# Intra-chunk decay masks of a state-space scan: rows read back from DRAM and masked by GpSimd selects, instead of float32r matmuls on TensorE

## The chip, the core and the metric

One NeuronCore of a Trainium2 chip runs the whole program as a single launch. Its engines are TensorE (PE, with weight loads as PEld), VectorE (DVE), ScalarE (ACT), GpSimd (POOL) and SyncE (SP, which here only issues DMAs). Each engine runs its own instructions in order and waits on semaphores for the others. The metric is the device time of one execution in microseconds (us).

## The reference, cut to what matters

One layer: adaLN and an input projection split into three head groups (a bidirectional Mamba-2 scan, pooling, neighbourhood attention), an output projection, then a PEER expert FFN and a final norm. The sequence has 512 tokens, that is 4 chunks of 128; the scan has 16 heads and two directions. Only this part of the scan is touched:

```python
def segsum(a):
    t = a.shape[-1]
    cs = jnp.cumsum(a, axis=-1)
    diff = cs[..., :, None] - cs[..., None, :]
    mask = jnp.tril(jnp.ones((t, t), dtype=bool))
    return jnp.where(mask, diff, -jnp.inf)
...
    lmat = jnp.exp(segsum(a))
    cb = jnp.einsum('bclhn,bcshn->bhcls', cc, bc)
    y_diag = jnp.einsum('bhcls,bcshp->bclhp', cb * lmat, xd)
```

For every chunk, head and direction a 128x128 matrix of log decays is needed, whose entry is the difference of two cumulated sums, with the wrong triangle at minus infinity. It goes through an exponential, is multiplied with `cb`, and weighs the tokens of the chunk.

## The kernel before, in words

The stage that the change touches runs from about 216 to 368 us of the span. It is written out by hand as 61 numbered steps (`at(step, f, ...)`, run in order of steps, and within a step in the order of the calls); every engine receives its instructions in that order. Three things are interleaved in it:

- The z, v and q projections: 16 pieces of weights (`p_load`, `p_split`), each loaded by SP into one of 3 `wraw` buffers, split by ACT (`wh`, L212) and DVE (`wl`, L215) into a high and a low float32r part, and used by 3 matmuls of 512 columns for each pair of operands (`mm3`, L222 to L224). About one fourth of a piece is done in each step.
- The chunk states (`st_in`, `st_mm`, `st_add`): DVE forms `xd` (L919) in one step, TensorE multiplies it in the next (L926), DVE adds in the one after that (L937), all in a chain.
- The within-chunk work. For chunk `c` (0 to 3) and unit `u` (0 to 3; four heads each), with `b = 4 + 10 * c`: `u_mm` in step `b+2u+1`, `u_exp` in `b+2u+2`, `u_mul` in `b+2u+3`, `u_diag` in `b+2u+5`. So there are 16 units, each two steps apart, and a pause of two steps between chunks.

In `u_mm` TensorE makes the masked cumulated sums of four heads, for both directions, in two PSUM banks: a product of a 128x128 matrix `steps[x]` with `rows` (128 x 2048, the identity times -2^100 in 112 partitions, and the cumulated sums, split in high and low, in the other 16), then a small product with `negs` for the last 16 columns (L969, L970). `u_exp` has ACT take the exponential with a bias for each head (L979, L982; 8 instructions of 128 columns). `u_mul` is two tensor_tensor instructions on DVE (L987: the two directions are added; L988: times `cb`). `u_diag` is four matmuls of 64 columns (L997). GpSimd has one instruction for each chunk in this stage, `y_init` (L1003). The constants `steps` (GpSimd, L912), `rows` (ACT, L901, and a DMA, L903), `idr` and `negs` (DVE, L905 and L909) are made once, at the stage's beginning. The cumulated sums come from two small matmuls, are split by ACT and DVE (L767, L768) and written to DRAM as `cs_d` (L770).

The last 20 steps (about 326 to 368 us) hold the gating, the norm and the transposes of the scan's output, and the q projection. Attention, the output projection and the FFN follow; they are not touched.

Of the kernel before, what the change touches and what calls it, by code (L numbers as in the profile page):

```python
# [7 lines left out]
F32 = mybir.dt.float32  # L8
F32R = mybir.dt.float32r
# [3 lines left out]
AF = mybir.ActivationFunctionType  # L13
ALU = mybir.AluOpType
# [3 lines left out]
P = 128  # L18
# [12 lines left out]
MASKED = -1.0e30  # L31
# [14 lines left out]


C_ID, C_U, C_L, C_SU, C_SL, C_ONE = 0, 128, 256, 384, 512, 640
C_X, NCST = 768, 784


def _consts():
    c = np.zeros((P, NCST), np.float32)
    k = np.arange(P)[:, None]
    m = np.arange(P)[None, :]
    c[:, C_ID:C_ID + P] = k == m
    c[:, C_U:C_U + P] = k <= m
    c[:, C_L:C_L + P] = k >= m
    c[:, C_SU:C_SU + P] = k > m
    c[:, C_SL:C_SL + P] = k < m  # L60
    c[:, C_ONE:C_ONE + P] = 1.0
    c[:, C_X:C_X + 8] = (k - 112 == m[:, :8]) | (k - 120 == m[:, :8])
    c[:, C_X + 8:C_X + 9] = k < 112
    return c


# [93 lines left out]
def build(tc, A, out, dbg=None):  # L160
    nc = tc.nc
    V, S, G, PE = nc.vector, nc.scalar, nc.gpsimd, nc.tensor
# [104 lines left out]
    cst = pers.tile([P, NCST], F32, name="cst")  # L267
    nc.scalar.dma_start(cst[:, 0:P], A["cst"][:, 0:P])
    ident = cst[:, C_ID:C_ID + P]
    U_in, L_in = cst[:, C_U:C_U + P], cst[:, C_L:C_L + P]  # L270
    SU, SL, ONE = cst[:, C_SU:C_SU + P], cst[:, C_SL:C_SL + P], cst[:, C_ONE:C_ONE + P]
# [483 lines left out]
    def decays(specs):  # L755
# [4 lines left out]
        for i, (_, _, t) in enumerate(specs):  # L760
            tc.keep_in_program_order(S.activation(t.rearrange("p t h -> p (t h)"), ps[:, i * HC:(i + 1) * HC], AF.Exp))
        return ps
    csT = [ad1.tile([NX * NH, 2, P], F32R, name=f"csT{i}") for i in range(2)]
    pcs = psG.tile([P, 512], F32, name="acc")[0:NX * NH, 0:2 * P].rearrange("p (d t) -> p d t", d=2)
    for d, m in enumerate((U_in, L_in)):
        tc.keep_in_program_order(PE.matmul(pcs[:, d, :], an[:, d, 0:NX, :].rearrange("p t h -> p (t h)"), m, start=True, stop=True))
    S.activation(csT[0], pcs, AF.Copy)  # L767
    V.tensor_tensor(csT[1], pcs, csT[0].bitcast(F32), ALU.subtract)  # L768
    for i in range(2):
        nc.scalar.dma_start(cs_d[i].rearrange("d p t -> p d t"), csT[i].bitcast(F32))  # L770
    decays([(SU, 0, enF), (SL, 1, enB), (ONE, 0, toF)])
    pin = decays([(ONE, 1, toB), (U_in, 0, inF), (L_in, 1, inB)])
    for d in range(2):
# [34 lines left out]
    def at(step, f, *a):  # L808
        plan.setdefault(step, []).append((f, a))
# [86 lines left out]
    def half_of(g):  # L896
        return slice(g * 512, (g + 1) * 512), slice(g * 8, (g + 1) * 8)
    SB = m1.tile([P, 4, D], F32, name="SB")
    rows = m1.tile([P, NH * P], F32R, name="rows")
    for i in range(4):  # L900
        S.activation(rows[0:112, i * 512:(i + 1) * 512].rearrange("p (h t) -> p h t", t=P), ident[0:112].unsqueeze(1).broadcast_to([112, 4, P]),  # L901
                     AF.Copy, scale=-2.0 ** 100)
    nc.scalar.dma_start(rows[112:P].bitcast(F32), cs_d.rearrange("i d (c h) t -> (i d c) (h t)", c=NX))  # L903
    idr = m1.tile([P, P], F32R, name="idr")
    V.tensor_copy(idr, ident)  # L905
    negs, steps = [], []
    for d, m in enumerate((SU, SL)):
        negs.append(m1.tile([P, 16], F32R, name=f"neg{d}"))
        V.tensor_scalar(negs[d], m[:, 112:P], -1e30, None, ALU.mult)  # L909
    for x in range(8):  # L910
        steps.append(m1.tile([P, P], F32R, name=f"steps{x}"))
        G.tensor_scalar(steps[x], (SL, SU)[x // 4], cst[:, C_X + 8:C_X + 9], cst[:, C_X + x:C_X + x + 1], ALU.mult, ALU.add)  # L912
    st, tmp = {}, {}


# [45 lines left out]
        for g in range(2):  # L961
            cbm[g, "r"] = cb[:, g, :]

    def u_mm(c, u):
        un[c, u] = []
        for d in range(2):
            ps = psM.tile([P, 512], F32, name="mm") if d else psT.tile([P, 4, P], F32, name="pt").rearrange("p a b -> p (a b)")
            x = 4 * d + c
            PE.matmul(ps, steps[x], rows[:, u * 512:(u + 1) * 512], start=True, stop=False)  # L969
            PE.matmul(ps.rearrange("p (a b) -> p a b", a=4)[:, :, 112:P], idr, negs[d].unsqueeze(1).broadcast_to([P, 4, 16]), start=False, stop=True)  # L970
            un[c, u].append(ps)

    def u_exp(c, u):
        pf, pb = un[c, u]
        t1 = m2.tile([P, 4, P], F32, name="t1", bufs=3)
        t2 = m2.tile([P, 4, P], F32, name="t2")
        for j in range(4):
            h = u * 4 + j
            S.activation(t1[:, j, :], pf[:, j * P:(j + 1) * P], AF.Exp, bias=ncs[0][:, c, h:h + 1])  # L979
        for j in range(4):  # L980
            h = u * 4 + j
            S.activation(t2[:, j, :], pb[:, j * P:(j + 1) * P], AF.Exp, bias=ncs[1][:, c, h:h + 1])  # L982
        un[c, u] = [t1, t2]

    def u_mul(c, u):
# [84 lines left out]
    for c in range(4):  # L1070
        b = U0 + UP * c
        at(b - 2, c_mm, c)
        at(b - 1, c_copy, c)
        for u in range(4):
            at(b + 2 * u + 5, u_diag, c, u)
            at(b + 2 * u + 1, u_mm, c, u)
            at(b + 2 * u + 2, u_exp, c, u)
            at(b + 2 * u + 3, u_mul, c, u)
        at(b + 1, y_init, c)
        at(b + 8, y_add, c, 0)  # L1080
        at(b + 12, y_add, c, 1)
# [1154 lines left out]
```

## Time and profile before

| | |
|---|---|
| runs of the kernel before | 1728.9, 1728.95, 1731.65 us, median 1728.95 |
| the profiled execution | 1730.5 us, of which the span from the first to the last instruction is 1728.7 us |
| mean granted TensorE clock | 0.997 |
| the touched stage | about 216 to 368 us of the span |

In the profile's rows a line stands for one group of instructions: line of the kernel, engine, operation, what it writes and reads, shape. In a timeline, the first column is the start in us from the span's start, the second the duration in us; the bracket at the end is the idle time of the engine before it and what ended it. In a table of windows, each engine has its busy us and the number of instructions.

### The profile page before, as it was taken

The numbers are of one execution on the slowest core, as the hardware profiler recorded it, in microseconds if no ns is written. First come the engines' busy times: TensorE is split into PE (matmuls) and PEld (weight loads), VectorE is DVE, ScalarE is ACT, GpSimd is POOL, SyncE is SP. The second block draws the span as 40 slices with busy tenths as digits, with TensorE's granted clock in tenths as the row PEclk, the third lists the DMA queues.
The fourth block names the chain that finished last, engine by engine and source line by source line (L and its number), as shares of the span: only waits on it lengthen the run. The fifth ranks groups of instructions, "written<-read, shape, count | busy, mean of one in ns | idle before, by whom it ended". The sixth has DMA issues, their size and how long they took to land.

```text
span 1728.7 us, 26484 instructions
## 1 busy us (share of the span) xinstructions
PE 1709.1 (99%) x9620; PEld 1482.9 (86%) x9620; DVE 1399.3 (81%) x2672; ACT 836.8 (48%) x1511; POOL 364.0 (21%) x283
## 2 busy tenths in 40 slices
PE   9999999999999999999999999999999999999998
PEld 7888777776789889999999999888888888888886
DVE  6688467886546599888989997988988989889886
ACT  5442345556535333556676764444444444444444
POOL 0003210012236444132121211222221212211200
PEclk9999999999999999999999999999999999999999
DMA  9457532375536434587999999999999999999972
GB/s 374 131 152 233 163 98 73 129 256 172 171 118 190 119 115 131 169 295 258 340 339 356 341 328 343 391 396 368 389 369 378 372 414 380 382 371 379 390 274 108
DMA packets 195634, 464.88 MB, mean 269 GB/s; under 512 B 14600, under 2 KB 118760, under 8 KB 177536
## 3 DMA queue, kind: packets, MB, share of 16 engines
q1 hardware_dynamic: 146976, 260.03, 43.6%
q0 software_dynamic: 21136, 144.83, 21.9%
q10 hardware_dynamic: 27392, 58.34, 9.1%
q8 instruction: 75, 1.23, 0.3%
q14 instruction: 55, 0.45, 0.1%
HBM read 409.92 MB, written 55.32 MB: 269 GB/s over the span
## 4 chain that ended last, share of the span: by engine, by line
PE 81%; DVE 8%; ACT 4%; DMA 3%; issue 2%; ACTq 1%; POOL 0%; SPq 0%; DVEq 0%; POOLq 0%
PE pv L224 10%; PE pv L223 10%; PE pv L222 10%; PE pu L224 7%; PE pu L222 7%; PE pu L223 7%; PE acc L222 5%; PE acc L223 5%; PE acc L224 5%; DMA act_d<-act 3%; DVE wl L215 2%; PE acc L461 1%; PE acc L466 1%; PE acc L463 1%; PE sps L1180 1%
## 5 line engine op out<-in xcount | busy, mean ns | idle before, releaser
L215 DVE TENSOR_TENSOR wl<-wraw,wh 128x1024 fp32r<-128x1024 f32 x295 | 361.3, 1236 | 97.6 <-ACT wh L212 95.9
L212 ACT ACTIVATE wh<-wraw 128x1024 fp32r<-128x1024 f32 x328 | 342.1, 1054 | 194.8 <-PE acc L223 75.6
L222 PE MATMUL pu<-u2h,wh 128*128 128x368 f32 x1008 | 336.8, 334 | 1.5 <-ACT act L1530 1.3
L224 PE MATMUL pu<-u2h,wl 128*128 128x368 f32 x1008 | 332.3, 330 | 1.5 <-DVE wl L215 1.5
L223 PE MATMUL pu<-u2l,wh 128*128 128x368 f32 x1008 | 331.8, 329 | 0.0
L224 PE MATMUL pv<-wh,wwl 128*128 128x512 f32 x768 | 299.3, 390 | 0.0
L223 PE MATMUL pv<-wl,wwh 128*128 128x512 f32 x768 | 299.1, 390 | 0.0
L222 PE MATMUL pv<-wh,wwh 128*128 128x512 f32 x768 | 299.0, 389 | 0.1
L1809 POOL DMA_INDIRECT row<-in_peer_uv,idxG x128 | 159.3, 1245 | 615.7 <-DVE accG L1823 577.0
L222 PEld LDWEIGHTS pu<-u2h,wh 128*128 128x128 f32 x1008 | 189.6, 188 | 3.4 <-ACT act L1530 1.7
L224 PEld LDWEIGHTS pu<-u2h,wl 128*128 128x128 f32 x1008 | 189.6, 188 | 2.8 <-DVE wl L215 2.7
L223 PEld LDWEIGHTS pu<-u2l,wh 128*128 128x128 f32 x1008 | 189.7, 188 | 1.4
L212 ACT ACTIVATE wwh<-gd 128x384 fp32r<-128x384 f32 x124 | 65.1, 525 | 242.8 <-DVE gd L2054 227.5
L224 PEld LDWEIGHTS pv<-wh,wwl 128*128 128x128 f32 x768 | 144.1, 188 | 30.4 <-DVE wwl L215 0.3
L222 PEld LDWEIGHTS pv<-wh,wwh 128*128 128x128 f32 x768 | 144.2, 188 | 29.3 <-ACT wwh L212 0.5
L223 PEld LDWEIGHTS pv<-wl,wwh 128*128 128x128 f32 x768 | 144.1, 188 | 29.1
L1823 DVE SCALAR_TENSOR_TENSOR accG<-row,wG,accG 128x1024 f32<-128x1024 f32 x127 | 162.4, 1279 | 1.6
L1814 DVE CUSTOM_DVE_ANT_0 row<-row,u2G 128x1024 f32<-128x1024 f32 x128 | 154.8, 1218 | 0.0
L1897 ACT ACTIVATE stg<-gdps 128x512 f32<-128x512 f32 x96 | 100.9, 1159 | 19.8 <-ACT act L1530 14.1
L215 POOL TENSOR_TENSOR wl<-wraw,wh 128x1024 fp32r<-128x1024 f32 x33 | 79.1, 2402 | 101.7 <-ACT wh L212 71.0
L1530 ACT ACTIVATE act<-pu 128x368 f32<-128x368 f32 x90 | 42.7, 474 | 107.7 <-PE pu L224 52.4
L215 DVE TENSOR_TENSOR wwl<-gd,wwh 128x384 fp32r<-128x384 f32 x124 | 68.9, 556 | 21.9 <-ACT wwh L212 21.9
(493 smaller groups left out, 3016.1 us busy)
## 6 DMA issues: line engine op xcount, KB each, us to landing
wraw<-in_peer_ut SPq DMA_DIRECT2D x128, 512.0 KB
wraw<-in_peer_uv SPq DMA_DIRECT2D x128, 512.0 KB
gd<-gd_d SPq DMA_DIRECT2D x15, 1536.0 KB
gd_d<-stg ACTq DMA_DIRECT2D x11, 2048.0 KB
wraw<-in_w_in SPq DMA_DIRECT2D x40, 512.0 KB
acl<-act_d SPq DMA_DIRECT2D x92, 184.0 KB
act_d<-act ACTq DMA_DIRECT2D x90, 184.0 KB
wraw<-in_w_out SPq DMA_DIRECT2D x16, 512.0 KB
```

What stands on the lines that cost most here:

```text
L212: S.activation(hi, full, AF.Copy)
L215: (eng or V).tensor_tensor(lo, full, hi.bitcast(F32), ALU.subtract)
L222: PE.matmul(ps, ah, bh, start=start, stop=False)
L223: PE.matmul(ps, ah, bl, start=False, stop=False)
L224: PE.matmul(ps, al, bh, start=False, stop=stop)
L461: PE.matmul(px, h[:, k, :], uh[:, k, :], start=s, stop=False)
L463: PE.matmul(px, h[:, k, :], ul[:, k, :], start=False, stop=False)
L1530: S.activation(act, pu[:, :TU], AF.Gelu)
L1809: G.indirect_dma_start(out=rows[k], out_offset=None, in_=A["peer_uv"], in_offset=bass.IndirectOffsetOnAxis(ap=idxG[:, k:k + 1], axis=0))
L1814: V.tensor_tensor_reduce(row[:, 0:D], row[:, 0:D], u2G, 1.0, 0.0, ALU.mult, ALU.add, actG[:, k:k + 1])
L1823: V.scalar_tensor_tensor(accG, row[:, D:2 * D], wG[:, k:k + 1], accG, ALU.mult, ALU.add)
L1897: S.activation(stg[:, :, t0:t0 + 4].rearrange("p a t -> p t a"), ps, AF.Copy, scale=1.0 if full else 1.0 / GSCALE)
```

## The change

`u_mm` and all that feeds it alone (`rows`, `idr`, `negs`, `steps`, the split of the cumulated sums, the constants `C_X`) are taken out. In its place, `u_load` has SP issue two DMAs for each unit (one for each direction): a row of 4 x 128 cumulated sums in `cs_d` is read 128 times, so that it lands in all partitions of an SBUF tile `cs0` or `cs1` (128 x 512, 256 KB; 3 buffers each). `u_mask` has GpSimd overwrite the wrong triangle of the tile with -1e30, by one affine_select for each direction, in place. `u_exp` reads the tile from SBUF. The load stands in step `b+2u-2`, the select in `b+2u`; `u_exp`, `u_mul` and `u_diag` keep their steps.

```diff
-C_X, NCST = 768, 784
+NCST = 768
...
-    cs_d = tc.dram_tile([2, 2, NX * NH, P], F32, name="cs_d")
+    cs_d = tc.dram_tile([2, NX * NH, P], F32, name="cs_d")
...
-    csT = [ad1.tile([NX * NH, 2, P], F32R, name=f"csT{i}") for i in range(2)]
+    csT = ad1.tile([NX * NH, 2, P], F32, name="csT")
...
-    S.activation(csT[0], pcs, AF.Copy)
-    V.tensor_tensor(csT[1], pcs, csT[0].bitcast(F32), ALU.subtract)
-    for i in range(2):
-        nc.scalar.dma_start(cs_d[i].rearrange("d p t -> p d t"), csT[i].bitcast(F32))
+    S.activation(csT, pcs, AF.Copy)
+    nc.scalar.dma_start(cs_d.rearrange("d p t -> p d t"), csT)
...
-    rows = m1.tile([P, NH * P], F32R, name="rows")
-    for i in range(4):
-        S.activation(rows[0:112, i * 512:(i + 1) * 512].rearrange("p (h t) -> p h t", t=P), ident[0:112].unsqueeze(1).broadcast_to([112, 4, P]),
-                     AF.Copy, scale=-2.0 ** 100)
-    nc.scalar.dma_start(rows[112:P].bitcast(F32), cs_d.rearrange("i d (c h) t -> (i d c) (h t)", c=NX))
-    idr = m1.tile([P, P], F32R, name="idr")
-    V.tensor_copy(idr, ident)
-    negs, steps = [], []
-    for d, m in enumerate((SU, SL)):
-        negs.append(m1.tile([P, 16], F32R, name=f"neg{d}"))
-        V.tensor_scalar(negs[d], m[:, 112:P], -1e30, None, ALU.mult)
-    for x in range(8):
-        steps.append(m1.tile([P, P], F32R, name=f"steps{x}"))
-        G.tensor_scalar(steps[x], (SL, SU)[x // 4], cst[:, C_X + 8:C_X + 9], cst[:, C_X + x:C_X + x + 1], ALU.mult, ALU.add)
...
-    def u_mm(c, u):
+    def u_load(c, u):
         un[c, u] = []
         for d in range(2):
-            ps = psM.tile([P, 512], F32, name="mm") if d else psT.tile([P, 4, P], F32, name="pt").rearrange("p a b -> p (a b)")
-            x = 4 * d + c
-            PE.matmul(ps, steps[x], rows[:, u * 512:(u + 1) * 512], start=True, stop=False)
-            PE.matmul(ps.rearrange("p (a b) -> p a b", a=4)[:, :, 112:P], idr, negs[d].unsqueeze(1).broadcast_to([P, 4, 16]), start=False, stop=True)
-            un[c, u].append(ps)
+            cs = m2.tile([P, 4, P], F32, name=f"cs{d}", bufs=3)
+            row = cs_d[d, c * NH + u * 4:c * NH + u * 4 + 4, :].rearrange("h t -> (h t)").unsqueeze(0)
+            nc.sync.dma_start(cs.rearrange("p h t -> p (h t)"), row.broadcast_to([P, 512]))
+            un[c, u].append(cs)
+
+    def u_mask(c, u):
+        for d, cs in enumerate(un[c, u]):
+            G.affine_select(cs, cs, pattern=[[0, 4], [1 - 2 * d, P]], compare_op=ALU.is_ge, fill=MASKED, base=0, channel_multiplier=2 * d - 1)
...
-            at(b + 2 * u + 1, u_mm, c, u)
+            at(b + 2 * u - 2, u_load, c, u)
+            at(b + 2 * u, u_mask, c, u)
             at(b + 2 * u + 2, u_exp, c, u)
```

On GpSimd, at the beginning of the stage, before: the last two of the eight `steps`, then the four `y_init` in a row (they wait only for their inputs), then what belongs to attention.

```order
L912 TENSOR_SCALAR steps_2150<-cst 128x128
L912 TENSOR_SCALAR steps_2152<-cst 128x128
L1003 TENSOR_TENSOR y<-xsn,rowv 128x1024 x2
L1003 TENSOR_TENSOR xsn<-xsn,rowv 128x1024 x2
L1203 TENSOR_SCALAR pr<-pr,sm 128x512 x16
```

The same place after (L956 is the select of `u_mask`, L988 is `y_init`; `cs0` and `cs1` are the two directions):

```order
L956 AFFINE_SELECT cs0_2166<-cs0_2166 128x512
L956 AFFINE_SELECT cs1_2168<-cs1_2168 128x512
L988 TENSOR_TENSOR y_2214<-xsn_128,rowv_70 128x1024
L956 AFFINE_SELECT cs0_2201<-cs0_2201 128x512
L956 AFFINE_SELECT cs1_2203<-cs1_2203 128x512
L956 AFFINE_SELECT cs0_2241<-cs0_2241 128x512
L956 AFFINE_SELECT cs1_2243<-cs1_2243 128x512
L956 AFFINE_SELECT cs0_2287<-cs0_2287 128x512
L956 AFFINE_SELECT cs1_2289<-cs1_2289 128x512
L956 AFFINE_SELECT cs0_2375<-cs0_2375 128x512
L956 AFFINE_SELECT cs1_2377<-cs1_2377 128x512
L988 TENSOR_TENSOR y_2453<-xsn_128,rowv_70 128x1024
```

Eight selects for each chunk now stand between one `y_init` and the next, 32 in all, and each `y_init` is queued behind selects, which wait for DMAs.

On TensorE, the first unit of the first chunk, before: the four products of `u_mm` between two groups of the z projection.

```order
L224 MATMUL acc<-wh,ul 128x512
L969 MATMUL pt<-rows,steps_2138 128x512
L970 MATMUL pt<-neg_2134,idr 128x4x16
L969 MATMUL mm<-rows,steps_2146 128x512
L970 MATMUL mm<-neg_2136,idr 128x4x16
L222 MATMUL acc<-wh,uh 128x512
L223 MATMUL acc<-wl,uh 128x512
```

The same place after, up to the next product of the chunk states (the line numbers of the file are lower by 2 in `mm3`, by 18 at `st_mm`):

```order
L222 MATMUL acc<-wh,ul 128x512
L220 MATMUL acc<-wh,uh 128x512
L221 MATMUL acc<-wl,uh 128x512
L222 MATMUL acc<-wh,ul 128x512
L908 MATMUL mm<-xd,Bn 128x512
```

The 64 products are gone from TensorE, and nothing else moved there in this stage.

On SP, before: the weight pieces of the stage stand one after the other.

```order
L579 DMA mod_d<-mod 1x512 x4
L243 DMA wraw<-in_w_in 128x2x512 x11
L243 DMA wraw<-in_w_in 128x8x128 x2
L1028 DMA SB<-zs_d 128x512 x4
L1028 DMA t_3083<-zs_d 128x512
```

After (L951 is the DMA of `u_load`, L241 that of a weight piece):

```order
L577 DMA mod_d<-mod 1x512 x4
L241 DMA wraw<-in_w_in 128x2x512 x2
L951 DMA cs_2166<-cs_d 128x512
L951 DMA cs_2168<-cs_d 128x512
L241 DMA wraw<-in_w_in 128x2x512
L951 DMA cs_2201<-cs_d 128x512
L951 DMA cs_2203<-cs_d 128x512
L951 DMA cs_2241<-cs_d 128x512
L951 DMA cs_2243<-cs_d 128x512
L241 DMA wraw<-in_w_in 128x2x512
L951 DMA cs_2287<-cs_d 128x512
L951 DMA cs_2289<-cs_d 128x512
```

The 32 loads of rows share SP's queue with the weight pieces. A load of unit `u` waits until ACT has read the tile of three units earlier, and the weight pieces behind it wait with it.

More of the change, by code (lines that the diff above doesn't have):

```diff
@@ L61, in _consts @@
     c[:, C_ONE:C_ONE + P] = 1.0
-    c[:, C_X:C_X + 8] = (k - 112 == m[:, :8]) | (k - 120 == m[:, :8])
-    c[:, C_X + 8:C_X + 9] = k < 112
     return c
@@ L978, in u_exp @@
             h = u * 4 + j
-            S.activation(t1[:, j, :], pf[:, j * P:(j + 1) * P], AF.Exp, bias=ncs[0][:, c, h:h + 1])
+            S.activation(t1[:, j, :], pf[:, j, :], AF.Exp, bias=ncs[0][:, c, h:h + 1])
         for j in range(4):
             h = u * 4 + j
-            S.activation(t2[:, j, :], pb[:, j * P:(j + 1) * P], AF.Exp, bias=ncs[1][:, c, h:h + 1])
+            S.activation(t2[:, j, :], pb[:, j, :], AF.Exp, bias=ncs[1][:, c, h:h + 1])
         un[c, u] = [t1, t2]
```

## The prediction

> **What bounds the kernel now.** I read the page first, then the busy time by stretches of the touched stage, then the timelines of TensorE, DVE and GpSimd in it, and at last other places where GpSimd and DVE meet.
>
> ```profile
> span 1728.7 us, 26484 instructions
> PE 1709.1 (99%) x9620; PEld 1482.9 (86%) x9620; DVE 1399.3 (81%) x2672; ACT 836.8 (48%) x1511; POOL 364.0 (21%) x283
> ```
>
> TensorE is never idle for long, so what leaves TensorE is worth its full time, as long as nothing else becomes late. The stage itself, cut at the first product of `u_mm` of each chunk (228.5, 254.9, 279.8, 308.6 us) and at the end of the within-chunk work:
>
> ```profile
> 228.50:254.90 26.40, 26.40 (x130) 20.80 (x129) 17.20 (x24) 14.93 (x41) 2.29 (x1) 1.00 0.29 89
> 254.90:279.80 24.90, 24.90 (x123) 19.58 (x123) 19.36 (x30) 10.60 (x34) 2.29 (x1) 1.00 0.24 65
> 279.80:308.60 28.80, 28.80 (x135) 21.82 (x135) 22.32 (x33) 13.80 (x39) 0.00 (x0) 1.00 0.35 106
> 308.60:340.00 31.40, 31.40 (x140) 22.84 (x139) 26.33 (x39) 20.63 (x52) 0.00 (x0) 1.00 0.31 105
> 340.00:368.00 28.00, 27.16 (x125) 19.97 (x123) 23.60 (x43) 13.64 (x27) 0.00 (x0) 1.00 0.71 235
> ```
>
> The columns after the comma are PE, PEld, DVE, ACT, POOL (busy us and instructions), the clock, the DMA share and GB/s. TensorE is busy all the time up to 340 us, at full clock; DVE is second, and grows from 65% to 84%; ACT, GpSimd and the DMA engines have room. So TensorE sets the pace, with DVE 5 to 9 us behind it in each stretch.
>
> **What the change removes.** One `u_mm` on TensorE, with its neighbours:
>
> ```profile
> 228.51 0.39 PE L969 MATMUL pt<-rows,steps 128*128 128x512 f32 x1
> 228.74 0.19 PE L970 MATMUL pt<-neg,idr 128*128 128x64 f32 x1
> 228.77 0.47 PE L969 MATMUL mm<-rows,steps 128*128 128x512 f32 x1
> 229.08 0.19 PE L970 MATMUL mm<-neg,idr 128*128 128x64 f32 x1
> 229.11 0.47 PE L222 MATMUL acc<-wh,uh 128*128 128x512 f32 x1
> 229.42 0.39 PE L223 MATMUL acc<-wl,uh 128*128 128x512 f32 x1
> 229.65 0.40 PE L224 MATMUL acc<-wh,ul 128*128 128x512 f32 x1
> ...
> 232.82 0.40 PE L969 MATMUL pt<-rows,steps 128*128 128x512 f32 x1
> ```
>
> From start to start the four products take 0.60 us, and the product behind them takes 0.31 where its neighbour takes 0.23: 0.68 us for a unit, 2.7 us for a chunk, 10.9 us for 16 units. The making of `rows`, `steps`, `idr` and `negs` goes too. It lies ahead of the first unit, beside the projections on TensorE:
>
> ```profile
> 210.00:220.00 10.00, 9.39 (x44) 7.60 (x43) 7.40 (x10) 5.15 (x7) 6.97 (x7) 1.00 0.59 170
> ```
>
> TensorE is idle for 0.61 us there, for whatever reason, so no more than that could be gained; I count it at zero.
>
> If nothing else changed, the stretches would be 23.7, 22.2, 26.1 and 28.7 us long.
>
> **What it adds: loads.** 32 loads of 256 KB are 8.4 MB in about 100 us, on DMA engines that are a third busy. A transfer of that size, from issue to the release of its buffer:
>
> ```profile
> 246.41 0.34 ACTq L834 DMA_DIRECT2D zs_d<-ztl  x1
> 250.78 0.60 ACT L833 ACTIVATE ztl<-acc 128x512 f32<-128x512 f32 x1 [2.90 <-DMA zs_d<-ztl]
> ...
> 259.56 1.14 ACT L979 ACTIVATE t<-pt,ncs 128x128 f32<-128x128 f32 x4 [2.13 <-PE pt L970]
> 260.57 1.16 ACT L982 ACTIVATE t<-mm,ncs 128x128 f32<-128x128 f32 x4
> ```
>
> 4.4 us. A tile comes round after three units: two issues (0.7), landing (4.4), two selects, each as long as the multiplication below (1.57) and behind one DVE instruction (0.6), and eight exponentials (2.2 from the last two rows) make 11.7 us; three units last about 13 (4.31 between the first two `u_mm`, from 228.51 to 232.82). The loads are hidden with little over 1 us to spare. The weight pieces behind them on SP are asked for 5 steps ahead of their split, so they are not near. Zero, then, and what happens when it fails is a rival.
>
> **What it adds: selects on GpSimd.** 32 of them, of 128x512. GpSimd has the time: 8 selects of up to 1.6 us and one `y_init` in 22 us. But it does not run beside DVE:
>
> ```profile
> 241.95 2.29 POOL L1003 TENSOR_TENSOR xsn<-xsn,rowv 128x1024 f32<-128x1024 f32 x1 [22.49 <-DVE xd L919]
> 242.50 2.27 DVE L988 TENSOR_TENSOR t<-t,cb 128x512 f32<-128x512 f32 x1
> 247.75 0.69 DVE L988 TENSOR_TENSOR t<-t,cb 128x512 f32<-128x512 f32 x1
> ```
>
> The same DVE instruction takes 0.69 us alone and 2.27 us when GpSimd's `y_init` has begun before it: it ends 0.53 us after GpSimd has, so it had stood still for 1.58 us. The other way round, and in alternation:
>
> ```profile
> 162.96 1.07 POOL L719 TENSOR_TENSOR pa<-pl 128x527 f32<-128x527 f32 x1 [3.12 <-ACT pl L717]
> 163.93 1.28 DVE L563 SCALAR_TENSOR_TENSOR adac<-qT,cc,adac 128x1024 f32<-128x1024 f32 x1 [1.91 <-DMA qT<-in_ada_w]
> 164.11 2.03 POOL L722 TENSOR_TENSOR pb<-pa 128x524 f32<-128x524 f32 x1
> 165.13 2.08 DVE L215 TENSOR_TENSOR wl<-wraw,wh 128x1024 fp32r<-128x1024 f32 x1
> ```
>
> GpSimd's second add waits for DVE's instruction, DVE's next one (1.22 us alone) waits 0.86 us for GpSimd's. They exclude each other where DVE reads two SBUF operands. Not where one is in PSUM: these DVE groups of 228.5 to 340 us are free of it.
>
> ```profile
> L937 DVE TENSOR_TENSOR SB<-SB,mm 128x512 f32<-128x512 f32 x8 | 5.5, 685 | 3.7 <-PE mm L926 3.4
> L937 DVE TENSOR_TENSOR sfw<-sfw,mm 128x512 f32<-128x512 f32 x7 | 4.8, 684 | 2.5 <-PE mm L926 2.4
> L1013 DVE TENSOR_TENSOR ytmp<-mm,inF 128x512 f32<-128x512 f32 x6 | 4.1, 686 | 1.3 <-PE mm L1008 1.3
> L1013 DVE TENSOR_TENSOR ytmp<-mm,inB 128x512 f32<-128x512 f32 x5 | 3.4, 686 | 1.2 <-PE mm L1008 1.2
> L1018 DVE TENSOR_TENSOR y<-y,yd 128x512 f32<-128x512 f32 x4 | 2.7, 678 | 0.0
> L1018 DVE TENSOR_TENSOR xsn<-xsn,yd 128x512 f32<-128x512 f32 x3 | 2.1, 685 | 1.8 <-PE yd L997 1.8
> L960 DVE COPY cb<-mm 128x256 f32<-128x256 f32 x3 | 1.3, 425 | 0.3
> ```
>
> Together 23.9 of 85.2 us (the DVE column of the four stretches); as neighbours overlap a little, one fourth. So three fourths of DVE's work stands still while a select holds the port.
>
> How long does a select hold it? Call it L. No select is in this trace. The nearest rows are one-input instructions of GpSimd:
>
> ```profile
> L1203 POOL TENSOR_SCALAR pr<-pr,sm 128x512 f32<-128x512 f32 x16 | 25.0, 1565 | 177.0 <-DVE sm L1202 164.2 <-PE sps L1180 8.2 <-DVE mn L1189 4.6
> 385.18 1.56 POOL L1203 TENSOR_SCALAR pr<-pr,sm 128x512 f32<-128x512 f32 x1 [3.74 <-DVE sm L1202]
> 386.28 1.23 DVE L215 TENSOR_TENSOR wl<-wraw,wh 128x1024 fp32r<-128x1024 f32 x1 [1.27 <-ACT wh L212]
> 873.47 0.97 POOL L1901 COPY mod<-stg 128x128 f32<-128x128 f32 x1 [1.94 <-ACT stg L1897]
> 874.21 1.31 DVE L1873 TENSOR_TENSOR oi<-iotaA,ixT 128x2048 f16<-128x2048 f16 x1
> 816.27 1.22 DVE L1873 TENSOR_TENSOR oi<-iotaA,ixT 128x2048 f16<-128x2048 f16 x1
> ```
>
> The multiplication by a column has exactly the select's shape and takes 1.565 us; a `wl` that began 1.10 us into it was not held (1.23), so L is at most 1.10 there. The copy of 128 columns held DVE for 0.09 us (1.31 against 1.22), 0.36 for 512. The two-input add above held it for 0.86. So L lies between 0.36 and 1.57 (the whole of the nearest instruction). A select computes a condition for each element, so I put it with the multiplication and above the add: **L = 1.0**.
>
> Then in each chunk DVE has its own work, 8 selects x 0.75 x L = 6.0 us of standing still, and 0.75 x 1.58 = 1.2 for its `y_init`. Its own work is 17.20 - 1.58 = 15.6 in the first stretch, then 19.4, 22.3, 26.3. With that it needs 22.8, 26.6, 29.5 and 33.5 us, against 23.7, 22.2, 26.1 and 28.7 of TensorE. The first stretch still goes at TensorE's pace (-2.7); the others go at DVE's: +1.7, +0.7, +2.1. Sum +1.8. An engine does not run dry of waits at 100%: where DVE was 84% busy, in the last stretch above, TensorE lost 0.84 of 28.0 us, so I add 3% of the 89.6 us that DVE now rules, 2.7. In all +4.5: what is late next, once TensorE has less to do, is `xd`, `wl` and the products with `cb`, for which TensorE waits in `st_mm`, the z projection and `u_diag`. Behind 340 us no select is left, and that part shifts as a whole.
>
> The profiled execution took 1730.5, so 1735.0 by its clock; the median of the runs is 1.55 lower: 1733.5 us.
>
> **A rule weighed.** The Trainium skill's GPSIMD Engine Reference (Engine selection) has one-input work on GpSimd "roughly line-rate" with DVE. By that page's 1.2 GHz, 512 elements would be an estimated 0.43 us, near the copy's 0.36 and far from the 1.565 us of the multiplication, which is the only row of this shape; by it the sum would be that of the first rival. The page SBUF — State Buffer (SBUF: two separate sides) says that the pair of ports is held for the full instruction and the loser fully blocks. The rows at 386.28 differ: there DVE went ahead 0.46 us before GpSimd's end. By the page the sum would be that of the third rival.
>
> **The rivals.**
>
> 1. *The selects let go early, and TensorE's gain stays.* With L = 0.36 DVE stands still 2.2 us a chunk and needs 19.0, 22.8, 25.7 and 29.7: -2.7, -2.1, -2.7, -1.7, and 3% of the 52.5 us that DVE rules is 1.6: -7.6, 1721.4 us. With no holding at all -10.9, 1718.0. For it speaks the copy, against it the multiplication of the same shape. It decides below L = 0.57, where the gain is over 0.2%. Chance 24%.
> 2. *The port eats the gain and no more.* L = 0.7: -2.7, -0.1, -1.1, +0.3 and 2.5: -1.1, 1727.9 us. Together with the lower part of my case (L up to 0.94, +3.4), within 0.2%: 26%.
> 3. *The port is held for the whole select.* L = 1.57: 9.4 us a chunk: 26.2, 30.0, 32.9, 36.9, that is -0.2, +5.1, +4.1, +5.5 and 3.8: +18.3, 1747.3 us. For it speaks `y_init`, which held DVE almost to its end; against it 386.28. From L = 1.2 on; chance 18%.
> 4. *The loads come late*: a landing over 5.7 us makes the round of three tiles longer than three units; ACT then waits for GpSimd, and SP holds back the weight pieces. At 8 us, some 2.3 us for three units, 12 us in all on top of rival 2: 1740 us. Nothing in the windows shows DMA engines that full; 4%.
>
> **The numbers.** My case (L from 0.94 to 1.2) has 28%, and is slower. A difference under 0.2%, 3.5 us, is about what can't be told from none here. Faster by more: rival 1, 24%. Within: 26%. Slower: 28 + 18 + 4 = 50%. The range reaches from 1720 (rival 1, without its very end) to 1748 (rival 3); what lies outside, no holding at all or selects of over 1.6 us, has some 15 to 20%.
>
> **What would show it.** Right: DVE's instructions with two SBUF operands (L987, L988, `xd`, `wl` by their new lines) have means well above 0.69 and 1.22 us in the stage, those with a PSUM operand have not; DVE is over 95% busy between 250 and 340 us, and TensorE shows waits for DVE there where it had none; the select's row is 1.1 to 1.6 us. Wrong: TensorE still 100% busy and the stage's end some 10 us earlier (rival 1); ACT's exponentials waiting long for GpSimd or for DMAs (rival 4); or a change of time outside 216 to 368 us.

## The result, and the profile after

The changed kernel takes 1718.41 us (median of 6 runs, 1715.91 to 1722.26) against 1728.93 us of the kernel before (6 runs): a ratio of 0.9948 with a 95% interval of 0.9932 to 0.9963. It is faster by some 10 us, where 4.5 us slower was forecast. Measured a second time it had a median of 1721.87 us against 1727.41 (0.9957, 0.994 to 0.9973). Its profiled execution took 1722.26 us.

```profile
span 1720.5 us, 26491 instructions
PE 1698.8 (99%) x9556; PEld 1473.3 (86%) x9556; DVE 1406.3 (82%) x2668; ACT 839.4 (49%) x1507; POOL 385.8 (22%) x307
```

TensorE's busy time fell by 10.3 us, and VectorE's and GpSimd's rose by 7 and 22. For the touched stage alone I take the time from the first product of `xd` with `Bn` to the first attention score, from TensorE's timeline; the rows of before, and then of after:

```profile
222.21 1.02 PE L926 MATMUL mm<-xd,Bn 128*128 128x512 f32 x2
368.28 0.49 PE L1180 MATMUL sps<-kT,qT 64*128 64x256 f32 x2
```

```profile
222.60 0.59 PE L908 MATMUL mm<-xd,Bn 128*128 128x512 f32 x1
361.14 0.49 PE L1166 MATMUL sps<-kT,qT 64*128 64x256 f32 x2
```

So 146.1 us before and 138.5 after (137.7 in the second profile): 7.5 to 8.4 us shorter. The spans of the two profiled executions differ by 8.2 us, so there nearly all of it is the stage. The medians differ by 2 to 3 us more than the stage does, and those of the second measurement by 2 to 3 us less; the other runs have no trace, so where that arises is not shown. The later stages are the same in all kernels here, but their times vary. The expert stage's first line of products runs for 249.3 us in the profile before and for 246.9 in that after, and in one of the experiments, whose kernel differs only ahead of it, for 240.9. The rows of before and of that experiment (`e7`):

```profile
L1894 PE MATMUL gdps<-ow,oi x384: 218/218/297, 794.8 to 1044.1; 128*128 128x128 f16 x184, 128*128 128x128 f32 x8
```

```profile
L1896 PE MATMUL gdps<-ow,oi x384: 218/218/280, 805.7 to 1046.6; 128*128 128x128 f16 x184, 128*128 128x128 f32 x8
```

That is why the experiments are read by the stage's length, which repeated within 0.9 us where a kernel was profiled twice, and their times only beside it.

The stretches after, cut by the lengths that the prediction gave for TensorE alone (23.7, 22.2, 26.1 and 28.7 us), in the columns of the table before:

```profile
228.50:252.20 23.70, 23.26 (x107) 17.64 (x106) 20.88 (x25) 16.36 (x45) 9.16 (x9) 1.00 0.65 199
252.20:274.40 22.20, 20.95 (x100) 15.59 (x100) 20.38 (x24) 13.23 (x40) 11.30 (x11) 1.00 0.61 171
274.40:300.50 26.10, 25.09 (x115) 18.63 (x114) 25.41 (x35) 15.03 (x39) 7.45 (x9) 1.00 0.63 175
300.50:329.20 28.70, 28.70 (x124) 20.47 (x123) 26.09 (x39) 15.77 (x37) 1.72 (x2) 1.00 0.37 114
```

TensorE now idles 0.4, 1.3 and 1.0 us in the first three and not at all in the fourth, and it waits for VectorE there (the groups of TensorE, 228.5 to 330 us):

```profile
L982 PE MATMUL yd<-xsn,t 128*128 128x64 f32 x120 | 15.3, 270 | 1.7 <-DVE y L1003 1.0 <-DVE t L973 0.7
L993 PE MATMUL mm<-sfw,CT 128*128 128x512 f32 x12 | 6.4, 614 | 1.0 <-DVE sfw L919 1.0
```

The timelines of GpSimd and of VectorE show the holding:

```profile
227.50 0.63 POOL L956 TENSOR_SCALAR_AFFINE_SELECT cs<-cs 128x512 f32<-128x512 f32 x1
...
237.47 0.86 POOL L956 TENSOR_SCALAR_AFFINE_SELECT cs<-cs 128x512 f32<-128x512 f32 x1 [1.57 <-DMA cs<-cs_d]
...
239.50 2.34 POOL L988 TENSOR_TENSOR y<-xsn,rowv 128x1024 f32<-128x1024 f32 x1
```

```profile
237.15 0.69 DVE L901 TENSOR_TENSOR xd<-xsn,enF 128x512 f32<-128x512 f32 x1
237.75 1.12 DVE L972 TENSOR_TENSOR t<-t,t 128x512 f32<-128x512 f32 x1
...
240.00 2.38 DVE L901 TENSOR_TENSOR xd<-xsn,enF 128x512 f32<-128x512 f32 x1
```

A select alone takes 0.63 us. The sum of `t`, 0.68 us alone, started behind a select and took 1.12: held for 0.44. The select had begun while VectorE's instruction before was still running (237.15 to 237.84) and took 0.86 us, so it had itself waited, and 0.44 is probably its whole holding and not the rest of one. `xd` behind `y_init` took 2.38: held for 1.70. Between 222 and 340 us, 23 of 81 instructions of VectorE with both operands in SBUF (128x512, those that the timeline shows singly) took 0.06 to 0.5 us over their 0.68, 0.37 on the mean, and three took 1.7 over it, behind `y_init` (two operands, 1024 columns). The groups of VectorE, 220 to 329 us:

```profile
L972 DVE TENSOR_TENSOR t<-t,t 128x512 f32<-128x512 f32 x16 | 13.9, 871 | 0.0
L973 DVE TENSOR_TENSOR t<-t,cb 128x512 f32<-128x512 f32 x16 | 13.8, 862 | 0.6
L901 DVE TENSOR_TENSOR xd<-xsn,enF 128x512 f32<-128x512 f32 x9 | 9.9, 1098 | 0.0
...
L919 DVE TENSOR_TENSOR SB<-SB,mm 128x512 f32<-128x512 f32 x8 | 5.5, 683 | 2.5 <-PE mm L908 2.1
...
L998 DVE TENSOR_TENSOR ytmp<-mm,inF 128x512 f32<-128x512 f32 x5 | 3.4, 683 | 0.2 <-PE mm L993 0.2
```

Those with an operand in PSUM (L919, L998) have 683 ns, as before (684 to 686); the others are longer.

### The profile page after: what moved, and what is told of

It reads as the page before. It is cut to its first block, busy times and chain, and to the rows that moved or that the text cites. A ratio compares the mean times of both kernels' runs of the same rounds, so it can differ in the third digit from the quotient of the medians.

```text
span 1720.5 us, 26491 instructions
## 1 busy us (share of the span) xinstructions
PE 1698.8 (99%) x9556; PEld 1473.3 (86%) x9556; DVE 1406.3 (82%) x2668; ACT 839.4 (49%) x1507; POOL 385.8 (22%) x307
## 4 chain that ended last, share of the span: by engine, by line
PE 82%; DVE 8%; DMA 3%; ACT 3%; issue 2%; ACTq 0%; SPq 0%; POOL 0%; DVEq 0%; POOLq 0%
PE pv L222 10%; PE pv L221 10%; PE pv L220 10%; PE pu L220 8%; PE pu L222 8%; PE pu L221 8%; PE acc L220 5%; PE acc L221 5%; PE acc L222 5%; DMA act_d<-act 3%; DVE wl L213 2%; PE acc L459 1%; PE acc L464 1%; PE acc L461 1%; PE sps L1166 1%
```

## The experiments

The theory at the outset: TensorE's 64 products were worth their full time, and the selects give part of it back by holding VectorE, some 0.4 us at a time. The rivals: the part given back is late loads; the gain is not TensorE's; holding does not reach the path. "Holds" in this table counts the instructions of VectorE as above, 0.06 to 1.3 us over 0.685, between 222 and 340 us. Ratios are to the kernel before, with the 95% interval.

| kernel | stage, us | holds, mean us | time, us | ratio |
|---|---|---|---|---|
| before | 146.1 | 0 | 1728.9 | |
| the change | 138.5; 137.7 | 23, 0.37; 20, 0.36 | 1718.4; 1721.9 | 0.9948 (0.9932 to 0.9963); 0.9957 (0.994 to 0.9973) |
| e1: no selects | 134.7 | 1, beside `y_init` | 1715.7 | 0.9939 (0.9916 to 0.9963) |
| e4: no selects, no loads | 134.7 | 0 | 1715.4 | 0.9939 (0.9921 to 0.9957) |
| e2: each select twice | 143.3 | 35, 0.41 | 1724.2 | 0.9983 (0.9971 to 0.9996) |
| e6: multiplication instead | 135.8 | 14, 0.35 | 1719.0 | 0.9951 (0.9932 to 0.997) |
| e10: two-input product instead | 150.7 | 27, 0.85 | 1734.2 | 1.0034 (1.0022 to 1.0047) |
| e5: memset instead | 136.4 | 3, all beside `y_init` | 1718.2 beside 1726.1, one run each | |
| e7: before, products twice | 156.7 | 0 | 1735.6 | 1.004 (1.0024 to 1.0056) |
| e3: before, with selects | 146.1 | 11, 0.36 | 1724.3 beside 1726.1, one run each | |
| e11, e15: select in 4 parts | 136.2; 136.6 | 25, 0.16 | 1717.6 | 0.9949 (0.9936 to 0.9962) |
| e14: select in 2 parts | 136.2 | 29, 0.17 | 1718.7 | 0.9942 (0.9929 to 0.9955) |

**What the products were worth, and whether loads cost.** `e1` takes the selects out, `e4` the loads as well, `e7` doubles the products of the kernel before, `e12` is the control for the edit of the exponentials.

```diff
 # e1 (and e4, with its exponentials reading two fixed tiles)
-            S.activation(t1[:, j, :], pf[:, j, :], AF.Exp, bias=ncs[0][:, c, h:h + 1])
+            S.activation(t1[:, j, :], pf[:, j, :], AF.Exp, bias=ONE[:, j:j + 1], scale=0.0)
...  (the same for t2)
-            at(b + 2 * u, u_mask, c, u)
 # e7, in before
+            PE.matmul(ps, steps[x], rows[:, u * 512:(u + 1) * 512], start=True, stop=False)
+            PE.matmul(ps.rearrange("p (a b) -> p a b", a=4)[:, :, 112:P], idr, negs[d].unsqueeze(1).broadcast_to([P, 4, 16]), start=False, stop=True)
```

> The changed kernel without its 32 selects; the exponentials read the loaded rows with scale 0 and bias 1, so the masking and the decays' values are left out and every instruction of ScalarE, VectorE and TensorE stays. Theory T (what the change gained is TensorE's 64 products, 10.9 us, and what it gave back of it is VectorE held by the selects, some 0.42 us for each VectorE instruction with two operands in SBUF): TensorE's idle time between 228 and 300 us, 2.7 us in the trace, goes for the larger part, so 1715.7 us (1714.5 to 1717.5), and the additions and multiplications of 512 columns in the decay work (0.87 us in the trace) fall back to 0.69. Rival A (what was given back is late loads): 1718.4, TensorE idle as before, additions at 0.69 all the same. Rival B (the selects cost nothing on the path because VectorE's longer instructions only fill its idle time): 1718.4.

> The changed kernel without its 32 selects and without the 32 loads; the exponentials read two tiles of zeros with scale 0 and bias 1, so the decays' values and the masking are left out. It is the kernel before with its 64 products taken out and nothing put in their place. Theory T (loads are hidden, price 0): the same as the kernel without selects within 1 us, 1715.7. If the 10.9 us of the 64 products were the whole of the change and nothing were given back, 1728.9 - 10.9 = 1718.0 is met at the latest here; a time above 1720 says that the gain isn't TensorE's. Rival A (loads cost): 1 to 3 us below the kernel without selects.

> The kernel before with each product of u_mm issued twice in a row; the result is the same. Theory T (TensorE is the bound there, and the 64 products are worth their own time of 0.68 us a unit): 10.9 us slower than the kernel before, 1738.9 us (1737 to 1741). Rival A (part of what left with the products was not TensorE's: buffers of PSUM, the making of the constants): 1729 to 1734.

> The changed kernel with its selects, and only the exponentials edited as in the runs that left the decays' values out (scale 0 and bias 1). A control: the edit should do nothing by itself, so the stage is 138.5 us as with the change (138 to 139), and not 134.7 as in the run without selects.

The windows of `e1`, at the same cuts:

```profile
228.50:252.20 23.70, 23.70 (x115) 18.42 (x114) 16.69 (x23) 15.53 (x42) 2.29 (x1) 1.00 0.67 189
252.20:274.40 22.20, 22.20 (x108) 17.18 (x108) 20.35 (x31) 14.30 (x42) 2.29 (x1) 1.00 0.64 202
274.40:300.50 26.10, 26.10 (x120) 19.45 (x120) 22.18 (x32) 14.28 (x39) 0.00 (x0) 1.00 0.65 183
```

TensorE has no idle time any more in these stretches, and the stage is 134.7 us with the loads and without them: they cost nothing here. Against before, 11.3 us are gone (10.9 were forecast for the products), and doubling the products adds 10.6 to the stage. The gain is TensorE's. Of it the change keeps 7.5 to 8.4, and 3.0 to 3.8 go to the selects: in the first profile of the change TensorE idles 3.1 us in the stage, all of it in waits for VectorE, against 0.4 in `e1`, and its 609 products are busy 1.1 us longer. `e7` met neither expectation by its time: by the medians it is only 6.7 us slower; in its profiled execution, of which the rows stand above, the expert stage is 8.4 us shorter than before, and the touched stage 10.6 us longer. What its other runs did there has no trace. The control's stage is 137.7, a little under the 138 to 139 that I expected but like the change's second one, so the edit of the exponentials does nothing that can be told.

**Whether the holding reaches the path.** `e2` issues each select twice; `e3` puts the same 32 selects, on tiles that nobody reads, into the kernel before.

```diff
 # e2 (e3 adds the same instruction to before, on two tiles of its own)
+            G.affine_select(cs, cs, pattern=[[0, 4], [1 - 2 * d, P]], compare_op=ALU.is_ge, fill=MASKED, base=0, channel_multiplier=2 * d - 1)
             G.affine_select(cs, cs, pattern=[[0, 4], [1 - 2 * d, P]], compare_op=ALU.is_ge, fill=MASKED, base=0, channel_multiplier=2 * d - 1)
```

> The changed kernel with each select issued twice in a row; the result is the same. Theory T: another 8 x 0.75 x 0.42 = 2.5 us of VectorE in each chunk of four, against room of 2.8, 1.8, 0.7 and 2.6 us (the stretch less VectorE's busy time): about 1 us comes through in the second chunk, 2 in the third and parts in the others, so 1722.5 us (1720 to 1727). Rival B (selects cost nothing on the path): 1718.4. Rival C (a select holds VectorE for as long as it lasts, 0.63 to 0.8 us): 8 x 0.75 x 0.75 = 4.5 us a chunk, so 1728 or more.

> The kernel before with its products kept, and 32 selects of GpSimd on two tiles that nobody reads, at the places that the change gives them; the result is the same. I read the stage's length in the trace, from the first product of xd with Bn to the first attention score: 146.1 us before, 138.5 with the change, 134.7 without selects. Theory T2 (a select holds VectorE some 0.4 us, and it costs only where VectorE then needs longer than TensorE): by the forecast's sum at L = 0.4 VectorE needs 19.2, 22.9, 25.8 and 29.8 us against 26.4, 24.9, 28.8 and 31.4 of TensorE, so 146.1 to 146.8. Rival D (each holding delays TensorE's work directly, in whichever kernel): 149 to 150, since the selects cost 3.8 us in the changed kernel.

Doubling costs 4.7 to 5.6 us more. Not all of that is waiting for VectorE: in this profile TensorE's granted clock was 0.50 for 3.4 us, from 300.0 to 303.4, while TensorE was the busy one (the clock is the third figure from the end).

```profile
300.00:303.20 3.20, 3.20 (x10) 2.40 (x8) 3.06 (x5) 0.04 (x1) 2.04 (x4) 0.50 0.57 165
303.60:310.00 6.40, 6.40 (x32) 4.66 (x31) 5.08 (x7) 0.00 (x0) 2.72 (x3) 1.00 0.55 162
```

At half the clock that is an estimated 1.7 us. It began 0.9 us after TensorE had waited 2.09 us for VectorE; but in `e10` a wait of 3.09 us (until 269.55) was followed by the full clock, so what lowered it stays open. The change, `e1` and before have 1.00 all through the stage.

In the kernel before the same selects cost nothing (146.1 us). Its windows:

```profile
228.50:254.90 26.40, 26.40 (x129) 20.73 (x128) 20.00 (x25) 14.90 (x41) 14.88 (x16) 1.00 0.31 99
254.90:279.80 24.90, 24.90 (x124) 19.57 (x124) 20.59 (x30) 10.58 (x34) 7.15 (x7) 1.00 0.23 66
```

VectorE's 17.20 of the first stretch has become 20.00, and TensorE's 26.40 covers it. The selects had all their inputs early in `e3`, so they ran sooner than in the change, and only 11 holds were counted, 4.0 us in all, against 23 and 8.5 in the change. So it is shown that these holds cost nothing under TensorE's cover; that 23 would cost nothing there too is not.

**What the length of a holding goes by.** This decides on the forecast's L. The select is replaced by the multiplication whose 1.565 us was my nearest row (`e6`), by a product of two tiles (`e10`), and by a memset, which reads nothing (`e5`).

```diff
-            G.affine_select(cs, cs, pattern=[[0, 4], [1 - 2 * d, P]], compare_op=ALU.is_ge, fill=MASKED, base=0, channel_multiplier=2 * d - 1)
+            G.tensor_scalar(cs, cs, ONE[:, 0:1], None, ALU.mult)   # e6
+            G.tensor_tensor(cs, cs, still[d], ALU.mult)            # e10
+            G.memset(cs, MASKED)                                   # e5
 # e6 and e10: the exponentials as in e1
```

> The changed kernel with each select replaced by GpSimd's multiplication of the same 128x512 tile by a column of ones, the shape whose 1.565 us was the nearest row of my forecast; exponentials with scale 0 and bias 1, so the masking and the decays' values are left out. Theory T (the forecast's sum was right and only the length of one holding was wrong): one multiplication holds VectorE for 1.0 to 1.4 us, 8 x 0.75 x 1.0 to 1.4 = 6 to 8.4 us a chunk; by the sum of the forecast 1733.5 at 1.0 and 24 us more for each us above, so 1733 to 1743. Rival B (what GpSimd does beside VectorE doesn't reach the path): 1718 to 1720, as with the selects.

> The changed kernel with each select replaced by GpSimd's product of the tile with a second tile of ones, the same 128x512 but with two inputs from SBUF; exponentials with scale 0 and bias 1, so the masking and the decays' values are left out. Theory T2, formed on the run with multiplications by a column (1719.0 us, where 1733 to 1743 was expected): a one-input instruction of GpSimd holds VectorE once, for some 0.4 us, whatever its own length is, while a two-input one holds it for most of its length. y_init held it 1.58 us with 1024 columns, so some 0.8 for 512: 4.8 us a chunk, about what two selects in a row cost (1724.2): 1725 us (1722 to 1729), and the additions with two SBUF operands that are hit take some 1.5 us. Rival D (every instruction of GpSimd holds VectorE about 0.4 us): 1718 to 1720.

> The changed kernel with each select replaced by a memset of the same tile: GpSimd writes 128x512 and reads nothing; the masking and the decays' values are left out. Theory T2 (the holding is for GpSimd's accesses to SBUF, and reading counts): less holding than a select, the stage 135 to 137.5 us. Rival E (any GpSimd instruction on the tile holds alike): 138 to 139.

My expectation for `e6` was wrong: 1719.0 us, not 1733 to 1743. The rows of GpSimd and VectorE:

```profile
232.73 1.91 POOL L956 TENSOR_SCALAR cs<-cs,cst 128x512 f32<-128x512 f32 x1 [0.50 <-DMA cs<-cs_d]
```

```profile
232.52 0.68 DVE L972 TENSOR_TENSOR t<-t,t 128x512 f32<-128x512 f32 x1
233.24 1.06 DVE L973 TENSOR_TENSOR t<-t,cb 128x512 f32<-128x512 f32 x1
234.23 1.21 DVE L213 TENSOR_TENSOR wl<-wraw,wh 128x1024 fp32r<-128x1024 f32 x1
```

The multiplication lasts 1.91 us and holds one VectorE instruction for 0.37; the next starts while it still runs (until 234.64) and is not held. GpSimd is busy much longer than it holds. With two inputs it is another matter (`e10`):

```profile
232.21 1.69 POOL L959 TENSOR_TENSOR cs<-cs,still 128x512 f32<-128x512 f32 x1 [0.61 <-ACT t L967]
```

```profile
232.07 0.68 DVE L975 TENSOR_TENSOR t<-t,t 128x512 f32<-128x512 f32 x1
232.79 1.66 DVE L976 TENSOR_TENSOR t<-t,cb 128x512 f32<-128x512 f32 x1
```

Held for 0.97 (of the 27 holds 19 are between 0.91 and 1.13), with less time on GpSimd than the multiplication (1.61 us on the mean of the 32 against 1.86). So this expectation was wrong as well: I had put some 0.8 us a hold and 1725 us (1722 to 1729), and 1734.2 were measured. And a memset holds nobody (`e5`):

```profile
237.08 0.53 POOL L956 MEMSET cs<- 128x512 f32 x1 [1.35 <-DMA cs<-cs_d]
```

```profile
236.57 0.69 DVE L901 TENSOR_TENSOR xd<-xsn,enF 128x512 f32<-128x512 f32 x1
237.17 0.68 DVE L972 TENSOR_TENSOR t<-t,t 128x512 f32<-128x512 f32 x1
```

Twelve such instructions of VectorE, with both operands in SBUF, start while a memset runs, and all take 0.68 or 0.69 us.

So over these four kinds of instruction L goes with what GpSimd reads, 0.37 us for one input of 512 columns and about 1 us for two, and not with how long it is busy. At the L of the two-input product the sum on record comes out: 4.5 us more than before were forecast for L = 1.0, and the stage is 4.6 longer, with 27 holds of 23.0 us together where the sum had 24. (The granted clock was 0.50 for some 3.3 us here too, from 243.9 to 247.3, in a stretch where VectorE was busy 23.13 of 23.70 us.)

The stage of `e5` is 136.4 us, as expected, but not the 134.7 of `e1`, though nothing holds VectorE there but `y_init`. What is late in it is shown with the parts.

**Whether parts hold less.** `e11` and `e15` cut each select into four of 128 columns, `e14` into two of 256; `e13` also cuts `y_init` into four.

```diff
-            G.affine_select(cs, cs, pattern=[[0, 4], [1 - 2 * d, P]], compare_op=ALU.is_ge, fill=MASKED, base=0, channel_multiplier=2 * d - 1)
+            for j in range(4):
+                G.affine_select(cs[:, j, :], cs[:, j, :], pattern=[[1 - 2 * d, P]], compare_op=ALU.is_ge, fill=MASKED, base=0, channel_multiplier=2 * d - 1)
 # e13 as well
-        G.tensor_tensor(hv(ys[c]), hv(xsn[:, c, :]), hbc(rowv[:, 64:80]), ALU.mult)
+        for j in range(4):
+            js = slice(j * 256, (j + 1) * 256)
+            G.tensor_tensor(hv(ys[c][:, js]), hv(xsn[:, c, js]), hbc(rowv[:, 64 + 4 * j:68 + 4 * j]), ALU.mult)
```

> The changed kernel with each select cut into four of 128 columns, one for each head; the result is the same. Theory T2 with the holding in proportion to the columns (the copy of 128 columns held VectorE 0.09 us, so 0.36 for 512): the stage within 1.5 us of the changed kernel's, 137.5 to 140. Rival F (a fixed holding of some 0.4 us for each instruction): four times the holding, 20 us in all four chunks, so 150 us or more.

> The selects in two parts of 256 columns; the result is the same. Theory T3: one part holds VectorE 0.18 to 0.2 us, so its instructions of 0.68 take 0.87 or so, and its standing still and the stage lie between one part and four: 136.5 to 138.2 us, time 1717.5. Rival F' (a holding has a fixed share for each instruction): 0.3 us or more for each part and a stage above 138.5.

> The four parts again, timed: stage 136.2 us (135.7 to 136.7) as in the look; time 2.4 us below the change's, which the noise of the later stages may hide: 1716 us (1714 to 1718).

> The selects in four parts of 128 columns, and y_init in four parts of 256 columns; the result is the same. Theory T3 (a GpSimd instruction that reads SBUF holds the port in proportion to the columns it reads and to its inputs, and lets VectorE in at its end): the xd hit by y_init takes some 1.1 us in place of 2.4, and the stage loses another 0.5 to 1 us against the four parts alone (136.2): 135.2 to 135.9, near the 134.7 without selects. Time 1716 us (1714 to 1718.5). Rival F (four parts of y_init hold four times as often for as long): 137 or more.

> The changed kernel as it is, beside the others on the same chip: stage 138.5 us (137.7 to 138.9, the spread to the control), time 1718.4 (1716.5 to 1720.5).

`e15` came out as expected. The stage of `e11` (136.2) is shorter than the 137.5 to 140 that I expected, that of `e14` (136.2) falls just below its range and that of `e13` (136.0) just above; the change's second time, 1721.9, lies above the 1716.5 to 1720.5. The timelines of VectorE, of `e14` and of `e11`, at the same instruction (0.68 us alone):

```profile
235.70 0.89 DVE L910 TENSOR_TENSOR SB<-sfw,toB 128x512 f32<-128x512 f32 x1
```

```profile
235.84 0.77 DVE L910 TENSOR_TENSOR SB<-sfw,toB 128x512 f32<-128x512 f32 x1
```

0.20 us for 256 columns and 0.09 for 128: about in proportion to the columns (of the 29 holds in `e14` 18 are 0.16 to 0.24, ten 0.09). VectorE gets in between two parts, so each of its instructions is held by one part at most as a rule, and the holds of `e11` sum to 4.0 us in place of 8.5: 22 of 0.06 to 0.12, and three beside `y_init` that make up half of the sum. In `e13` the parts of `y_init`, 256 columns of two inputs, hold for 0.27 to 0.49 in place of 1.7. The stage is 1.1 to 2.4 us shorter than with the change; `e13` comes to 136.0. The times (1717.6, 1718.7, and 1718.1 for `e13`) can't be told from the change's. All of them stay 1.2 us or more above `e1`. In `e14` TensorE still waits 1.17 us for `sfw`, behind an instruction that `y_init` held; in `e11`, `e13` and `e15` something else is late (`e11`; ScalarE, then VectorE, then TensorE):

```profile
251.24 0.60 ACT L829 ACTIVATE ztl<-acc 128x512 f32<-128x512 f32 x1 [5.15 <-DMA zs_d<-ztl]
...
252.24 1.06 ACT L210 ACTIVATE wh<-wraw 128x1024 fp32r<-128x1024 f32 x1 [0.40 <-ACT ztl L829]
```

```profile
253.33 1.22 DVE L213 TENSOR_TENSOR wl<-wraw,wh 128x1024 fp32r<-128x1024 f32 x1 [4.85 <-ACT wh L210]
254.47 0.68 DVE L919 TENSOR_TENSOR sfw<-sfw,mm 128x512 f32<-128x512 f32 x1
255.07 0.68 DVE L901 TENSOR_TENSOR xd<-xsn,enF 128x512 f32<-128x512 f32 x1
```

```profile
255.90 1.10 PE L908 MATMUL mm<-xd,Bn 128*128 128x512 f32 x2 [1.19 <-DVE xd L901]
```

ScalarE waits 5.15 us for the store of a z tile (2.90 before), and `wh`, `wl`, `xd` and TensorE wait behind it. The issues of this store and of the nearest weight piece (512 KB), in `e11` and then in the change, show a difference of order:

```profile
244.54 0.39 SPq L241 DMA_DIRECT2D wraw<-in_w_in  x1
244.61 0.35 ACTq L830 DMA_DIRECT2D zs_d<-ztl  x1
```

```profile
243.88 0.33 ACTq L830 DMA_DIRECT2D zs_d<-ztl  x1
245.62 0.38 SPq L241 DMA_DIRECT2D wraw<-in_w_in  x1
```

The piece waits until VectorE has finished an earlier `wl`, and here VectorE is held less (that `wl` ends at 243.56 us in `e11`, at 245.59 in the change). So the piece comes sooner and goes ahead of the store, behind two loads of rows. In all six runs where it went less than 0.1 us ahead (`e5`, `e8`, `e9`, `e11`, `e13`, `e15`) the store took 6.3 to 6.7 us from its issue to the release of its buffer, and TensorE then waited 0.9 to 1.3 us for `xd` at about 255 us. Where it went 0.9 us or more behind (both profiles of the change, `e2`, `e12`, `e14`) the store took 4.0 to 4.7, and TensorE had no such wait. In `e1`, 0.4 us behind, the store took 5.2, and TensorE did not wait. In the kernel before, without the loads, the piece went 0.47 ahead and the store took 4.4. That loads and piece together delay the store agrees with all these traces, but moving the piece wasn't tried.

**Two versions with `y_init` moved.** `e8` issues the first two `y_init` before the within-chunk work, `e9` also puts the copy of `cb` on ScalarE.

```diff
-        at(b + 1, y_init, c)
+        at(1 + c if c < 2 else b + 1, y_init, c)
 # e9 as well
-        V.tensor_copy(cb.rearrange("p a b -> p (a b)"), cbm.pop(c)[:, 0:2 * P])
+        S.activation(cb.rearrange("p a b -> p (a b)"), cbm.pop(c)[:, 0:2 * P], AF.Copy)
```

> The changed kernel with y_init of the first two chunks issued before the within-chunk work (steps 1 and 2 instead of 5 and 15); the result is the same. Theory T: the xd that takes 2.38 us at 240.0 us in the trace falls to 1.1 or less, and the one after 261.7 likewise; what they hold before 228 us falls on other work. 1717 us (1715.5 to 1719). Rival B (VectorE's waits don't reach the path): 1718.4, the same as the changed kernel.

> As the run with y_init early, and the copy of cb (0.42 us a chunk on VectorE) on ScalarE; the result is the same. Theory T: 0.4 us a chunk less on VectorE in the chunks that it rules: 1716.5 us (1715 to 1718.5). Against it: ScalarE has the copy behind its exponentials, and the products with cb wait for it; then 1718 or more.

1718.7 us (0.9942, 0.9923 to 0.9961) and 1720.8 (0.9951, 0.9935 to 0.9966), stages 137.9 and 139.0: no gain that can be told. The time of `e8` doesn't decide between its two expectations, and that of `e9` is what was named against it. In `e8` the `xd` at 240.3 us takes 1.11 us as expected, but the `y_init` at 261.7 us in the change is the third and was not moved. The early ones hold a `wl` and an `xd` ahead of the stage instead (2.08 us at 217.6, 2.39 at 219.6). TensorE has no idle time from 222.5 to 252.2 us, and then loses 1.2 us at about 255 us behind the late store.

## Why the prediction was wrong, point by point

- **TensorE sets the pace and its 64 products are worth 10.9 us: right.** 11.3 us by the stage of `e1`, 10.6 by that of `e7`.
- **Loads hidden, price zero: right** for the change (`e1` and `e4` have the same stage). Rival 4 falls. The store of a z tile, of which the forecast has no term, did come late in other versions.
- **GpSimd and VectorE exclude each other only where VectorE reads two SBUF operands: right, as far as it goes.** L919 and L998 keep 683 ns while L972 rises to 871. By `e5` GpSimd has to read as well. The forecast let three fourths of 32 selects meet such an instruction, 24; 23 holds were counted, 20 in the second profile, and 14 in `e6`.
- **L = 1.0: wrong, and this is the step that failed.** It measured 0.37 on the mean. The select's row, forecast at 1.1 to 1.6 us, is 0.63 alone and 0.87 on the mean of the 32. I had put the select with the multiplication of the same shape, because I took the length of an instruction on GpSimd for the length of its holding. `e6` shows that this very multiplication holds no longer than the select. The prediction had the right row in hand: the copy of 128 columns, 0.09 us, is the value that `e11` shows for 128 columns. The choice should have gone by the number of inputs read from SBUF, and there copy and select stand together, and the two-input add (0.86) and `y_init` apart. By the sum L = 0.36 gives 1721.4 us in place of 1733.5, so this one term turned a gain into a loss. That the median, 1718.4, lies lower still the stage does not account for.
- **The sum as a function of L: right in total, in part by luck.** The first rival's 7.6 us of gain at L = 0.36 stand against 7.5 and 8.4 in the stage. At the other end `e10` met the forecast's own number with the forecast's own L. But the sum gave each stretch eight selects and a `y_init`; GpSimd ran 9, 11, 9 and 2 instructions in the four. At L = 0.36 it lost 0.6 us in the second, 1.0 in the fourth and 1.6 by the 3%; TensorE's idle time was 0.4, 1.3, 1.0 and 0.0. The total fits better than its parts. The Trainium skill's GPSIMD Engine Reference (Engine selection), by which I worked out an estimated 0.43 us for one input, gave the better L; as a statement on duration it doesn't fit the 1.56 us that one multiplication takes alone in `e6`.
- **VectorE over 95% busy from 250 to 340 us: only in one stretch** (25.41 of 26.10 us; 84.09 of the 90). TensorE's waits for VectorE were there, as said, but 2.7 us of them.
- **The port held for the whole instruction (rival 3): falls**, by the 0.37 of 1.91 us in `e6`. The Trainium skill's SBUF — State Buffer (SBUF: two separate sides) has the pair held for the whole instruction; the rows of `e6` differ. The Trainium skill's SBUF — State Buffer (Who interferes with whom) says that a VectorE instruction with two SBUF inputs contends with a GpSimd instruction that reads SBUF and not with one that only writes it. The twelve instructions of `e5`, at 0.68 or 0.69 us, agree.

What stays open: why the stage of `e6`, whose holds are as long but fewer (14), is 2 to 3 us shorter than the change's. TensorE waits there only once for VectorE up to 340 us, 0.9 us for `sfw` at 293.2 us, behind an instruction that `y_init` held. A longer instruction on GpSimd leaves fewer starts to collide with, but which instruction is hit differs too, and this was not separated. Open as well are the lowered clock in `e2` and `e10`, and what the selects would cost if the z store's place were fixed.

## What to carry to other kernels

Price work on GpSimd beside a loaded VectorE by what it reads from SBUF, columns times inputs, and not by its duration; look in the trace for a VectorE instruction that started behind the nearest relative of the new one, and subtract its time alone. When rows disagree on a price, ask what sets it before choosing the nearest by shape. Put such work where another engine covers VectorE's longer time: the same 32 selects cost nothing in the kernel before (11 holds), and 3 to 4 us once TensorE was relieved (23 holds). And look at what a less held engine releases sooner: here a weight piece went ahead of a store, and took back about 1 us of what the shorter holds had won.

## What the runs showed of the hardware

- An affine_select of 128x512 float32 takes 0.63 us alone on GpSimd and holds a two-SBUF-operand instruction of VectorE for 0.3 to 0.45 us as a rule, one of 256 columns for up to about 0.2, one of 128 for 0.09 (the change, `e14`, `e11`).
- A multiplication by a column, 1.56 us alone and 1.86 on the mean, holds it for about 0.4 us as well (`e6`); a product of two tiles, 1.27 us alone and 1.61 on the mean, for about 1 us (`e10`); a memset (0.53 us) not at all (`e5`).
- A z store issued right behind two loads of 256 KB and a weight piece of 512 KB took 6.3 to 6.7 us from its issue to the release of its buffer, and 4.0 to 4.7 where the piece came 0.9 us or more behind it.
